# Two of the eight modulation groups of a diffusion trunk's first stage: off TensorE, onto VectorE and onto ScalarE with GpSimd

## The chip, the cores and the metric

The kernel runs on one core of a Trainium2 chip. The metric is the device time of one execution in microseconds, as the median over runs. Engines are named as in the profile: PE is TensorE (matmul; PEld its weight loads), DVE is VectorE, ACT is ScalarE, POOL is GpSimd, SP is the engine that issues most DMAs.

## The reference

The reference is a trunk of two layers over 512 latent tokens and 256 context tokens, width 2048, all in float32. Each layer normalises its input, scales and shifts it by vectors that come from a condition, and projects it. The part that matters here is the modulation of the first layer:

```python
c_act = jax.nn.silu(c)
cc_act = jax.nn.silu(c_ctx)
...
shift, scale, gate = jnp.split(c_act @ w_mod + b_mod, 3, axis=-1)
shift_c, scale_c, gate_c = jnp.split(cc_act @ w_mod + b_mod, 3, axis=-1)
...
hc = rms_norm(xc, norm_g) * (1 + scale_c) + shift_c
h = rms_norm(x, norm_g) * (1 + scale[:, None, :]) + shift[:, None, :]
p = h @ w_in
```

So two vectors of 2048 (one for latent, one for context tokens) are multiplied by the first 4096 columns of `w_mod` (2048 x 6144), 33.5 MB that are read once. Everything after it (pooling, neighbourhood attention, convolution, output projection) is left as it is by the change.

## The kernel before

`start` (L531) is the first stage. It loads x and the context, transposes them, and makes the first four blocks of the projection `h @ w_in` with the class `Multi` (L1583), eight PSUM accumulators at a time. The 16 slices k of h (128 channels each) become available two at a time, since slice k needs its shift and scale.

*Modulation groups.* `mod_first` (L338) makes the shift and scale of one pair of slices, j and j + 1: group j, for j = 0, 2, ... 14. A group has 16 tiles of `w_mod` of 128 x 512 floats (256 KB, L347), issued by SP into a ring of `WB` = 27 buffers with the tag `wm`. PE multiplies four tiles at a time, each in its own 32 columns of the array (L353, one *step*); four steps make a group. The trace has two records per tile, so a step is a row of x8. Then `row` copies the PSUM row to SBUF with DVE and ACT (L358, L359), and `columns` lets PE sum the four parts and turn the row into columns (L364, the *fold*), whereupon DVE adds the bias (L407 to L409).

*The modulate chain.* Behind the fold, `modulate` (L626) makes the two latent and two context slices: DVE multiplies (L632), ACT adds the shift and rounds to the high part (L636, `hil` or `hic`), DVE makes the low part (L637). DVE and ACT alternate, four times per group.

*The order.* Every engine executes its instructions in the order in which the Python code records them. `mod_order` puts the steps, rows and folds of the eight groups into one list `work`. For each pair of slices, `Multi.unit` runs over four blocks and calls `between` twice per block, after the latent and after the context matmuls: 8 x 4 x 2 = 64 *places*. At each place `between` (L675) takes as many entries of `work` as a table (`xs`, `ys`) says, so that group j's fold stands 7 places ahead of the pair that needs it (group 10's at place 33, group 12's at 41, group 14's at 49). A step is recorded with the loads of later tiles behind it (`load`), into the buffers which it frees.

*Weights.* The weight tiles `raw` of `w_in` (256 KB, L254) are loaded by SP in the same queue, converted by ACT (L298), and their low part made by POOL (L300) in this stage. Three matmuls per slice use them (`mm3`, L734 to L736).

*The later modulation.* `mod_rest` makes the gate and the second layer's modulation off PE already: DVE multiplies and adds (`mac`, L369 to L377), and `mod_sum` (L380) sums over partitions with eight matmuls (L384), `mod_row` copies (L390), and `mod_columns` transposes (L396).

Of the kernel before, what the change touches and what calls it, by code (L numbers as in the profile page):

```python
# [10 lines left out]
F32 = mybir.dt.float32  # L11
F32R = mybir.dt.float32r
I32 = mybir.dt.int32
AF = mybir.ActivationFunctionType
ALU = mybir.AluOpType
# [4 lines left out]
D = 2048  # L20
KT = 16
# [11 lines left out]

CONV_K = 31
NMULTI = 4
RAW = 4

MORE = (1, 3)
# [54 lines left out]
class Kernel:  # L93
# [84 lines left out]
    def setup(self):  # L178
# [21 lines left out]
        for l in range(2):  # L200
            bl = self.blocks(l)
            for u in range(4):
                self.order += [("in", l, col, u) for _, col, _ in bl[:NMULTI]]
            for name, col, _ in bl[NMULTI:]:
                if name not in "qkvg":
# [70 lines left out]
    def w_conv(self):  # L276
# [11 lines left out]
        else:  # L288
# [8 lines left out]
            else:  # L297
                nc.scalar.activation(out=hi, in_=t, func=AF.Copy)  # L298
                eng = nc.gpsimd if n < 4 * NMULTI else nc.vector
                eng.tensor_tensor(out=lo, in0=t, in1=hi.bitcast(F32), op=ALU.subtract)  # L300
# [36 lines left out]
    def mod_first(self, p, j, bufs):  # L337
# [29 lines left out]

        return ([lambda k=k: load(k) for k in range(KT)], [lambda k=k: mm(k) for k in range(0, KT, 4)], [row, columns])

    def mac(self, acc, wm, k):  # L370

        for r, a in enumerate(acc):
            w = self.cond[:, r, k:k + 1]
            if k == 0:
                self.nc.vector.tensor_scalar(out=a, in0=wm, scalar1=w, scalar2=None, op0=ALU.mult)
            else:
                self.nc.vector.scalar_tensor_tensor(out=a, in0=wm, scalar=w, in1=a, op0=ALU.mult, op1=ALU.add)  # L377
# [7 lines left out]
                                      start=r == 0, stop=r == len(acc) - 1)  # L385
        return ps

    def mod_row(self, p, ps):
        ms = p.tile([128, 128], F32, tag="ms", name="ms")
        self.nc.vector.tensor_copy(out=ms, in_=ps[:, :128])  # L390
        return ms

# [138 lines left out]

    def start(self, p):
        nc = self.nc
        WB = 27

        work = self.mod_order(p, WB, lambda k, cx: modulate(k, cx))
        loads = deque(f for w in work for f in w[0])

        def load(n=1):
            for _ in range(min(n, len(loads))):  # L540
                loads.popleft()()
# [4 lines left out]
        for c in range(4):  # L546
            for cx, c1 in ((False, c), (True, 2 * c), (True, 2 * c + 1)):
                for tb in (4, 5) if cx else range(4):
                    w = 256 if cx else 512
                    key = ("c" if cx else "l") + str(2 * c1 + tb - 4 if cx else 4 * c1 + tb)  # L550
                    t = self.ph.tile([128, w], F32, tag="hi" + key, name="x" + key)
                    src = self.ctx_in[0, (tb - 4) * 128:(tb - 3) * 128] if cx else self.x[0, tb * 128:(tb + 1) * 128]
# [2 lines left out]
        load(8)  # L555
        while self.n_load < RAW:
            self.w_load()
        load(12)
        self.cs = p.tile([128, KT, 32], F32, name="cs")
        self.zero = p.tile([128, 128], F32R, name="zero")  # L560
        nc.gpsimd.memset(self.cs, 0.0)
# [1 line left out]
        for r in range(2):  # L563
# [4 lines left out]
                                op=ALU.add)  # L568
# [79 lines left out]
                    if j == "row":  # L648
                        break

        load(WB - 20)
        go(2)

        nc.vector.tensor_reduce(out=self.st[:, 0, 0:6], in_=ssq, axis=AX.X, op=ALU.add)
        r = self.rstd(self.st[:, 0, 0:6], 6, 1.0 / D, EPS)
        rb = p.tile([128, NT], F32, name="rb")
        for a, n in ((0, 4), (4, 2)):
            d = p.tile([128, 128 * n], F32, tag="junk0", name="diag")
# [11 lines left out]
        total, i = len(work), 0  # L670
# [5 lines left out]
        def between():  # L676
            nonlocal i
            i += 1
            go(int(np.interp(i, xs, ys)) - total + len(work))

        for j in range(0, KT, 2):
            while j not in done:
                go()
            for b in range(NMULTI):
                m.unit(j // 4, b, (j, j + 1), between)
        return m

    def mod_order(self, p, bufs, modulate):

        work = deque()  # L690
        for j in range(0, KT, 2):
            ld, mm, (row, columns) = self.mod_first(p, j, bufs)
            work.extend((ld[4 * n:4 * n + 4], f, None) for n, f in enumerate(mm))
            work.append(((), row, "row"))

            def finish(j=j, columns=columns):
                columns()
                for cx in (False, True):
                    for k in (j, j + 1):
                        modulate(k, cx)  # L700

            work.append(((), finish, j))
        return work
# [959 lines left out]
```

## Time and profile before

| | |
|---|---|
| median of 3 runs | 2376.94 us (2376.27 to 2379.21) |
| the profiled execution | 2379.58 us, its span 2377.8 us |
| PE busy | 2333.8 us, 98% of the span |
| DVE, ACT, POOL busy | 1577.4, 907.7, 525.4 us |
| DMA | 384.96 MB, mean 162 GB/s; 316 and 343 GB/s in the first two of 40 slices (59 us each) |

The span is cut into 40 slices on the page; the first stage, of which the change speaks, fills the first two and most of the third. Busy time of PE is modelled, so a full PE need not be PE at its peak. Where a wait is put down to an engine, that is the one that came last by the profile.

### The profile page before, as it was taken

The numbers are of one execution on the slowest core, as the hardware profiler recorded it, in microseconds if no ns is written. First come the engines' busy times: TensorE is split into PE (matmuls) and PEld (weight loads), VectorE is DVE, ScalarE is ACT, GpSimd is POOL, SyncE is SP. The second block draws the span as 40 slices with busy tenths as digits, with TensorE's granted clock in tenths as the row PEclk, the third lists the DMA queues.
The fourth block names the chain that finished last, engine by engine and source line by source line (L and its number), as shares of the span: only waits on it lengthen the run. The fifth ranks groups of instructions, "written<-read, shape, count | busy, mean of one in ns | idle before, by whom it ended". The sixth has DMA issues, their size and how long they took to land. (4 is left out here: it accounts for less than half of the span.)

```text
span 2377.8 us, 35567 instructions
## 1 busy us (share of the span) xinstructions
PE 2333.8 (98%) x13020; PEld 1976.9 (83%) x13020; DVE 1577.4 (66%) x2815; ACT 907.7 (38%) x1798; POOL 525.4 (22%) x654
## 2 busy tenths in 40 slices
PE   7999999999999999999999999999999999999998
PEld 4578888888888888888787887878888888888888
DVE  4359995468777877877666387863666667555435
ACT  4233335233333333344522265544333334344323
POOL 1124554122212212211101122452111111010001
PEclk9999999999999999999999999999999999999999
DMA  9967787556355435535765347986555554334633
GB/s 316 343 184 186 166 209 165 154 149 160 99 152 152 137 103 157 159 100 165 240 205 164 125 148 172 207 183 162 150 139 138 149 146 127 102 89 123 202 120 129
DMA packets 377072, 384.96 MB, mean 162 GB/s; under 512 B 24672, under 2 KB 294080, under 8 KB 376768
## 3 DMA queue, kind: packets, MB, share of 16 engines
q1 hardware_dynamic: 339232, 290.92, 41.8%
q0 software_dynamic: 37664, 91.76, 16.8%
q8 instruction: 102, 1.67, 0.3%
q14 instruction: 74, 0.61, 0.1%
HBM read 296.57 MB, written 24.08 MB: 135 GB/s over the span
## 5 line engine op out<-in xcount | busy, mean ns | idle before, releaser
L734 PE MATMUL g<-hil,whi 128*128 128x512 f32 x1600 | 634.5, 397 | 0.0
L736 PE MATMUL g<-hil,wlo 128*128 128x512 f32 x1600 | 626.2, 391 | 6.3 <-DMA wlo<-raw 4.0
L735 PE MATMUL g<-lol,whi 128*128 128x512 f32 x1600 | 627.1, 392 | 0.0
L300 DVE TENSOR_TENSOR wlo<-raw,whi 128x512 fp32r<-128x512 f32 x424 | 308.7, 732 | 181.3 <-ACT whi L298 178.3
L298 ACT ACTIVATE whi<-raw 128x512 fp32r<-128x512 f32 x440 | 272.9, 625 | 359.0 <-PE g L735 125.9
L736 PEld LDWEIGHTS g<-hil,wlo 128*128 128x128 f32 x1600 | 300.8, 188 | 75.5 <-DMA wlo<-raw 5.9
L377 DVE SCALAR_TENSOR_TENSOR mod<-wm,cond,mod 128x512 f32<-128x512 f32 x420 | 338.6, 847 | 26.2 <-DMA wm<-in_w_mod_dram 25.8
L734 PEld LDWEIGHTS g<-hil,whi 128*128 128x128 f32 x1600 | 301.7, 189 | 60.0 <-issue 6.8
L735 PEld LDWEIGHTS g<-lol,whi 128*128 128x128 f32 x1600 | 301.7, 189 | 53.1 <-issue 1.4
L736 PE MATMUL g<-hic,wlo 128*128 128x256 f32 x1024 | 290.0, 283 | 0.0
L735 PE MATMUL g<-loc,whi 128*128 128x256 f32 x1024 | 289.9, 283 | 0.0
L734 PE MATMUL g<-hic,whi 128*128 128x256 f32 x1024 | 288.6, 282 | 0.0
L839 DVE SCALAR_TENSOR_TENSOR acc<-ypad,cols,acc 128x783 f32<-128x783 f32 (+1 forms) x240 | 241.6, 1007 | 7.4
L734 PEld LDWEIGHTS g<-hic,whi 128*128 128x128 f32 x1024 | 195.4, 191 | 9.4
L735 PEld LDWEIGHTS g<-loc,whi 128*128 128x128 f32 x1024 | 195.5, 191 | 9.3
L736 PEld LDWEIGHTS g<-hic,wlo 128*128 128x128 f32 x1024 | 195.5, 191 | 0.0
L1239 ACT ACTIVATE e<-e,m 128x512 f32<-128x512 f32 x128 | 92.6, 724 | 249.0 <-DVE m L1237 249.0
L295 POOL DMA_DIRECT2D wlo<-raw x128 | 114.7, 896 | 253.0 <-ACT wlo L294 213.5
L432 POOL DMA_DIRECT2D wm<-in_w_mod_dram x98 | 71.2, 726 | 340.3 <-DVE mod L377 256.3
L294 ACT ACTIVATE wlo<-raw 128x512 fp32r<-128x512 f32 x128 | 80.4, 628 | 127.3 <-PE g L736 122.2
L1463 POOL TENSOR_TENSOR xn<-xn,res 128x512 f32<-128x512 f32 (+1 forms) x34 | 45.9, 1358 | 332.4 <-DVE xn L1459 270.6
L434 POOL DMA_DIRECT2D wm<-in_w_mod_dram x88 | 48.3, 549 | 249.8 <-DVE mod L377 218.4
(324 smaller groups left out, 3812.9 us busy)
## 6 DMA issues: line engine op xcount, KB each, us to landing
raw<-in_w_in_dram SPq DMA_DIRECT2D x416, 256.0 KB, 3.8
wm<-in_w_mod_dram SPq DMA_DIRECT2D x198, 256.0 KB, 5.9
wm<-in_w_mod_dram POOLq DMA_DIRECT2D x186, 256.0 KB, 4.1
raw<-in_w_out_dram SPq DMA_DIRECT2D x160, 256.0 KB, 3.2
wlo<-raw POOLq DMA_DIRECT2D x128, 256.0 KB, 4.5
q<-parts SPq DMA_DIRECT2D x32, 384.0 KB, 8.7
k<-parts SPq DMA_DIRECT2D x64, 192.0 KB, 3.9
raw<-mixd SPq DMA_DIRECT2D x32, 256.0 KB, 3.1
```

Source lines behind the costliest of these rows:

```text
L294: nc.scalar.activation(out=lo, in_=t, func=AF.Copy, scale=-1.0)
L295: nc.gpsimd.dma_start(out=lo, in_=t, accum_op=ALU.add)
L298: nc.scalar.activation(out=hi, in_=t, func=AF.Copy)
L300: eng.tensor_tensor(out=lo, in0=t, in1=hi.bitcast(F32), op=ALU.subtract)
L377: self.nc.vector.scalar_tensor_tensor(out=a, in0=wm, scalar=w, in1=a, op0=ALU.mult, op1=ALU.add)
L432: self.wm_queue.dma_start(out=t.rearrange("p (s n) -> p s n", s=2), in_=src)
L434: self.wm_queue.dma_start(out=t, in_=rows[:, 2 * D + 512 * j:2 * D + 512 * j + 512])
L734: mm(ps, whi, hhi, start=start, stop=False)
L735: mm(ps, whi, hlo, start=False, stop=False)
L736: mm(ps, wlo, hhi, start=False, stop=stop)
L839: nc.vector.scalar_tensor_tensor(out=acc[i][:, 0:na], in0=y[:, j:j + na], scalar=w, in1=acc[i][:, 0:na], op0=ALU.mult, op1=ALU.add)
L1239: nc.scalar.activation(out=e, in_=e, func=AF.Exp, scale=-1.0, bias=m[:, 0:1], accum_out=m[:, 1:2])
```

## The change

Group 12 is summed by DVE (`"d"` in the table `SIDE`), group 14 by ACT and POOL (`"p"`). The new `mod_side` loads their 32 tiles with the name `ws`, through rings of 4 and 3 buffers, on SP. DVE takes two instructions per tile (one per condition, with `mac`). For the other group ACT writes two products per tile and POOL adds each to its sum. Both end with `mod_sum`, `mod_row` and `mod_columns`, as in `mod_rest`. Step k of a side group stands at place `int(at[k]) + 1`, evenly from 1 to 34 for group 12 and from 1 to 42 for group 14. Its four steps and fold on PE are gone; row and columns of both groups stay in `work`, which puts the sum matmuls at places 37 and 45 and the transposes at 41 and 49. The ring `wm` shrinks from 27 to 14 buffers, and two prefetches (`load(12)`, `load(WB - 20)`) become one (`load(6)`).

```diff
--- before.py
+++ after.py
@@ -33,6 +33,8 @@
 
 CONV_K = 31
 NMULTI = 4
+
+SIDE = {12: "d", 14: "p"}
 RAW = 4
 
 MORE = (1, 3)
@@ -367,6 +369,41 @@
 
         return ([lambda k=k: load(k) for k in range(KT)], [lambda k=k: mm(k) for k in range(0, KT, 4)], [row, columns])
 
+    def mod_side(self, p, j, eng, name):
+
+
+        nc = self.nc
+        bufs = 4 if eng is nc.vector else 3
+        wm, s = {}, {}
+        acc = [p.tile([128, 512], F32, name=f"{name}{r}") for r in range(2)]
+
+        def load(k):
+            if k < KT:
+                t = wm[k] = p.tile([128, 512], F32, tag=name, name="ws", bufs=bufs)
+                src = self.w_mod[0, k * 128:(k + 1) * 128, 0:2 * D].rearrange("p (s n) -> p s n", s=2)
+                nc.sync.dma_start(out=t.rearrange("p (s n) -> p s n", s=2), in_=src[:, :, 128 * j:128 * (j + 2)])
+
+        def step(k):
+            if k == 0:
+                for i in range(bufs - 1):
+                    load(i)
+            load(k + bufs - 1)
+            if eng is nc.vector:
+                self.mac(acc, wm.pop(k), k)
+                return
+            t = wm.pop(k)
+            for r in range(2):
+
+                x = p.tile([128, 512], F32, tag="wq", name="wq", bufs=2) if k else acc[r]
+                nc.scalar.activation(out=x, in_=t, func=AF.Copy, scale=self.cond[:, r, k:k + 1])
+                if k:
+                    eng.tensor_tensor(out=acc[r], in0=acc[r], in1=x, op=ALU.add)
+
+        def row():
+            s["ms"] = self.mod_row(p, self.mod_sum(acc), "ms" + name)
+
+        return ([lambda k=k: step(k) for k in range(KT)], [row, lambda: self.mod_columns(0, j, s["ms"], "t")])
+
     def mac(self, acc, wm, k):
 
         for r, a in enumerate(acc):
@@ -385,8 +422,8 @@
                                       start=r == 0, stop=r == len(acc) - 1)
         return ps
 
-    def mod_row(self, p, ps):
-        ms = p.tile([128, 128], F32, tag="ms", name="ms")
+    def mod_row(self, p, ps, tag="ms"):
+        ms = p.tile([128, 128], F32, tag=tag, name="ms")
         self.nc.vector.tensor_copy(out=ms, in_=ps[:, :128])
         return ms
 
@@ -531,7 +568,7 @@
 
     def start(self, p):
         nc = self.nc
-        WB = 27
+        WB = 14
 
         work = self.mod_order(p, WB, lambda k, cx: modulate(k, cx))
         loads = deque(f for w in work for f in w[0])
@@ -555,7 +592,7 @@
         load(8)
         while self.n_load < RAW:
             self.w_load()
-        load(12)
+        load(6)
         self.cs = p.tile([128, KT, 32], F32, name="cs")
         self.zero = p.tile([128, 128], F32R, name="zero")
         nc.gpsimd.memset(self.cs, 0.0)
@@ -648,7 +685,6 @@
                     if j == "row":
                         break
 
-        load(WB - 20)
         go(2)
 
         nc.vector.tensor_reduce(out=self.st[:, 0, 0:6], in_=ssq, axis=AX.X, op=ALU.add)
@@ -678,6 +714,12 @@
             i += 1
             go(int(np.interp(i, xs, ys)) - total + len(work))
 
+            for n, steps in enumerate(self.side):
+                at = np.linspace(0, 33 + 8 * n, KT)
+                for k in range(KT):
+                    if i - 1 == int(at[k]):
+                        steps[k]()
+
         for j in range(0, KT, 2):
             while j not in done:
                 go()
@@ -688,9 +730,14 @@
     def mod_order(self, p, bufs, modulate):
 
         work = deque()
+        self.side = []
         for j in range(0, KT, 2):
-            ld, mm, (row, columns) = self.mod_first(p, j, bufs)
-            work.extend((ld[4 * n:4 * n + 4], f, None) for n, f in enumerate(mm))
+            if j in SIDE:
+                steps, (row, columns) = self.mod_side(p, j, {"d": self.nc.vector, "p": self.nc.gpsimd}[SIDE[j]], "w" + SIDE[j])
+                self.side.append(steps)
+            else:
+                ld, mm, (row, columns) = self.mod_first(p, j, bufs)
+                work.extend((ld[4 * n:4 * n + 4], f, None) for n, f in enumerate(mm))
             work.append(((), row, "row"))
 
             def finish(j=j, columns=columns):
```

Counted from the first modulation tile, the 96th and last tile of groups 0 to 10 was SP's load 108 (96 of them and 12 of weights); now it is load 136 (96, 27 side tiles and 13 of weights). The 128 tiles and 16 weight tiles of the stage end with load 144 before, and the last side tile is load 144 now.

The queue of SP, before, from the loads behind group 0's last two steps on (`raw` weights, `wm` modulation tiles):

```order
L347 DMA wm<-in_w_mod_dram 128x2x256 x8
L254 DMA raw<-in_w_in_dram 128x4x128
L347 DMA wm<-in_w_mod_dram 128x2x256 x32
L254 DMA raw<-in_w_in_dram 128x4x128
L347 DMA wm<-in_w_mod_dram 128x2x256 x8
L254 DMA raw<-in_w_in_dram 128x4x128
L347 DMA wm<-in_w_mod_dram 128x2x256 x4
```

And now, from the loads behind group 2's steps on (`ws` are side tiles):

```order
L349 DMA wm<-in_w_mod_dram 128x2x256 x16
L384 DMA ws<-in_w_mod_dram 128x2x256 x7
L349 DMA wm<-in_w_mod_dram 128x2x256 x4
L384 DMA ws<-in_w_mod_dram 128x2x256 x2
L349 DMA wm<-in_w_mod_dram 128x2x256 x8
L384 DMA ws<-in_w_mod_dram 128x2x256 x2
L349 DMA wm<-in_w_mod_dram 128x2x256 x4
L384 DMA ws<-in_w_mod_dram 128x2x256 x3
L256 DMA raw<-in_w_in_dram 128x4x128
```

Side tiles now stand among the tiles of groups 4 to 10; 27 of the 32 are ahead of the last of these.

DVE around group 10's chain, before: the end of the chain (`lol`, `loc` low parts), then the copy of group 12's row and its bias:

```order
L637 SCALAR_TENSOR_TENSOR lol_1280<-xm,sh_78,hil_1279 128x512
L632 SCALAR_TENSOR_TENSOR xm<-xTc_406,gs_76,rb 128x256
L637 SCALAR_TENSOR_TENSOR loc_1286<-xm,sh_78,hic_1285 128x256
L632 SCALAR_TENSOR_TENSOR xm<-xTc_408,gs_76,rb 128x256
L637 SCALAR_TENSOR_TENSOR loc_1292<-xm,sh_78,hic_1291 128x256
L358 COPY ms<-pv 128x256
L407 TENSOR_TENSOR sh_78<-t,cols 128x2x2
```

And now, up to the copy of group 12's summed row (L427, of what PE's sum matmuls wrote):

```order
L674 SCALAR_TENSOR_TENSOR lol_1388<-xm,sh_78,hil_1387 128x512
L669 SCALAR_TENSOR_TENSOR xm<-xTc_398,gs_76,rb 128x256
L674 SCALAR_TENSOR_TENSOR loc_1394<-xm,sh_78,hic_1393 128x256
L669 SCALAR_TENSOR_TENSOR xm<-xTc_400,gs_76,rb 128x256
L674 SCALAR_TENSOR_TENSOR loc_1400<-xm,sh_78,hic_1399 128x256
L414 SCALAR_TENSOR_TENSOR wd_93<-ws,cond,wd_93 128x512
L414 SCALAR_TENSOR_TENSOR wd_94<-ws,cond,wd_94 128x512
L427 COPY ms<-pv 128x128
```

The last two products of the side sum (`wd`, L414) stand behind the whole chain, and ahead of the row that PE sums from them.

ACT around group 12's chain, before (`hil` and `hic` high parts, `ms` a row, `whi` weights):

```order
L359 ACTIVATE ms<-pv 128x256
L636 ACTIVATE hil_1383<-xm,sh_78 128x512
L636 ACTIVATE hil_1389<-xm,sh_78 128x512
L636 ACTIVATE hic_1395<-xm,sh_78 128x256
L636 ACTIVATE hic_1401<-xm,sh_78 128x256
L298 ACTIVATE whi<-raw 128x512 x3
L359 ACTIVATE ms<-pv 128x256
L298 ACTIVATE whi<-raw 128x512
L636 ACTIVATE hil_1507<-xm,sh_78 128x512
```

And now (`wq` the products that POOL adds):

```order
L398 ACTIVATE wq<-ws,cond 128x512 x6
L673 ACTIVATE hil_1493<-xm,sh_78 128x512
L673 ACTIVATE hil_1499<-xm,sh_78 128x512
L673 ACTIVATE hic_1505<-xm,sh_78 128x256
L673 ACTIVATE hic_1511<-xm,sh_78 128x256
L398 ACTIVATE wq<-ws,cond 128x512 x2
L300 ACTIVATE whi<-raw 128x512 x4
L673 ACTIVATE hil_1611<-xm,sh_78 128x512
```

The products of the last tile stand behind the four high parts of group 12, and the row copies of groups 12 and 14 on ACT are gone.

## Rows read from the trace of the kernel before

**Rows 1.** The page, part 1: busy time and share of the span.

```profile
PE 2333.8 (98%) x13020; PEld 1976.9 (83%) x13020; DVE 1577.4 (66%) x2815; ACT 907.7 (38%) x1798; POOL 525.4 (22%) x654
```

**Rows 2.** By stretch: length, busy engines, granted PE clock, DMA share, GB/s.

```profile
46.00:50.00 4.00, 4.00 (x8) 2.20 (x8) 2.64 (x5) 1.23 (x2) 0.00 (x0) 0.50 1.11 349
50.00:54.00 4.00, 4.00 (x33) 1.11 (x32) 1.19 (x3) 1.03 (x2) 1.28 (x1) 0.81 1.11 344
62.00:67.00 5.00, 4.75 (x20) 1.53 (x17) 1.36 (x3) 0.55 (x2) 0.00 (x0) 1.00 1.10 336
67.00:81.00 14.00, 14.00 (x89) 8.67 (x88) 5.19 (x12) 3.05 (x6) 0.00 (x0) 1.00 1.10 348
137.00:151.00 14.00, 14.00 (x88) 11.32 (x85) 5.51 (x12) 4.98 (x10) 5.04 (x4) 1.00 0.26 76
```

**Rows 3.** Timeline of SP, first stage: start, length, loads in a row.

```profile
29.41 20.36 SPq L347 DMA_DIRECT2D wm<-in_w_mod_dram  x27
...
59.85 23.82 SPq L347 DMA_DIRECT2D wm<-in_w_mod_dram  x32
...
100.28 11.60 SPq L347 DMA_DIRECT2D wm<-in_w_mod_dram  x16
...
127.53 3.53 SPq L347 DMA_DIRECT2D wm<-in_w_mod_dram  x5
```

**Rows 4.** Waits of SP's queue, 0 to 150: total us, times, longest.

```profile
SPq L347 <- DMA wm<-in_w_mod_dram: 28.2, 86, 0.8
...
SPq L347 <- PE pv L353: 5.6, 13, 1.1
```

**Rows 5.** Timeline of PE: wm steps (L353), folds (L364), first matmuls of pairs.

```profile
50.06 4.32 PE L353 MATMUL pv<-wm,cs 128*32 128x512 f32 x32
...
100.57 0.95 PE L364 MATMUL t<-fold,ms 128*128 128x2 f32 x8
...
111.42 1.07 PE L353 MATMUL pv<-wm,cs 128*32 128x512 f32 x8
...
114.63 0.95 PE L364 MATMUL t<-fold,ms 128*128 128x2 f32 x8
...
152.04 0.28 PE L734 MATMUL s<-hic,whi 128*128 128x256 f32 x1
...
160.44 0.39 PE L734 MATMUL g<-hil,whi 128*128 128x512 f32 x1
```

**Rows 6.** Timelines of PE and PEld: two waits, length and releaser.

```profile
45.92 0.80 PE L1601 MATMUL s<-hil,zero 128*128 128x512 f32 x1 [2.16 <-ACT hil L636]
...
65.97 0.14 PEld L353 LDWEIGHTS pv<-wm,cs 128*32 128x32 f32 x2 [1.16 <-DMA wm<-in_w_mod_dram]
```

**Rows 7.** PE timeline later; lines by form, 0 to 150; two lines (min/median/max).

```profile
285.68 0.64 PE L384 MATMUL pv<-mod,sel 128*32 128x128 f32 x16
286.25 0.50 PE L734 MATMUL g<-hil,whi 128*128 128x512 f32 x1
...
686.40 0.27 PE L396 MATMUL pv<-kc,ms 128*128 128x128 f32 x1
...
L300 POOL TENSOR_TENSOR wlo<-raw,whi 128x512 fp32r<-128x512 f32 x16 | 20.1, 1275 | 121.7 <-ACT whi L298 93.5 <-DMA wm<-in_w_mod_dram 28.3
...
L298 ACT ACTIVATE whi<-raw 128x512 fp32r<-128x512 f32 x16 | 9.4, 621 | 0.3
...
L377 DVE SCALAR_TENSOR_TENSOR mod<-wm,cond,mod x420: 737/746/3495, 174.1 to 2020.3; 128x512 f32<-128x512 f32 x140
...
L788 POOL TENSOR_TENSOR pwl<-pw,pwh x8: 1401/1582/1636, 203.0 to 1518.4; 128x512 fp32r<-128x512 f32 x8
```

**Rows 8.** Timelines of DVE and ACT: ends of one modulate chain.

```profile
115.61 0.17 DVE L407 TENSOR_TENSOR sh<-t,cols 128x4 f32<-128x4 f32 x1 [2.55 <-PE t L364]
...
123.01 0.48 DVE L637 SCALAR_TENSOR_TENSOR loc<-xm,sh,hic 128x256 fp32r<-128x256 f32 x1 [0.58 <-ACT hic L636]
...
122.47 0.51 ACT L636 ACTIVATE hic<-xm,sh 128x256 fp32r<-128x256 f32 x1 [0.95 <-DVE xm L632]
```

## Prediction

> **What bounds the kernel now.** I read the page first: PE is busy for 98% of the span [rows 1], so once the first stage is over whatever shifts PE shifts the end, and only the first 160 us need a closer look. Next came the busy time by stretch [rows 2]. The DMA share is at 1.10 to 1.11 with 336 to 349 GB/s in the stretches from 46 to 81 us, and in 137:151, when the modulation tiles are in, it falls to 0.26. So two things are at their limit in the same stage: PE, full from 67 us on, and the transfers, full until about 135 us.
>
> The queue of SP, in order of time, shows the same from the side of the loads [rows 3]. Count loads from the first modulation tile. Load 52 goes out at 59.85, and the 32 loads of that row take 23.82 us, 0.744 us each. Load 144, the last modulation tile, starts 0.37 us before its row ends, at 130.69: 92 intervals in 70.84 us, 0.770 each. SP spends 28.2 us in 86 waits for earlier modulation transfers and 5.6 us in 13 waits for PE to free a buffer [rows 4]: the transfers set the pace.
>
> PE's rows [rows 5] show how close PE runs behind. One group takes 14.06 us (fold at 100.57 to fold at 114.63). A pair of k without modulation work takes 8.40 us (152.04 to 160.44). So a group's four steps and its fold cost PE 5.66 us. Tile 44 was load 52, issued at 59.85, and PE's wait for it ended at 65.97 [rows 6]: landing is 6.1 us behind the issue. Tile 96, the last of group 10, is load 108, the fifth of the row at 100.28, so issued near 103.3 and landed near 109.4. PE begins that step at 111.42. The slack is 2 us.
>
> **The change, part by part.**
> *Work off PE.* Groups 12 and 14 lose eight steps and two folds: 2 x 5.66 = 11.3 us less. Each gets 16 sum records, 0.57 us from their start to the next matmul, and one transpose of 0.27 us [rows 7]: 2 x 0.84 = 1.7 us more. All of it is in PE's queue, so all of it counts: -9.6 us.
>
> *Order of the loads.* The bytes stay the same; their order does not. Steps of the side groups stand at places 1 to 34 and 1 to 42 of the stage's 64, and the paces of groups 0 to 10 are kept. So 27 side tiles and one more weight tile now go out ahead of tile 96: it is load 136, not 108. The sums that need these side tiles stand later, at places 37 and 45. Three groups (tiles 48 to 95) now span 73 loads, 24.3 per group, 18.2 us at 0.75, where PE needs 14.06: PE waits about 4 us in each. Landing of tile 96 from load 52: 65.97 + 84 x 0.75 = 129.0. To this comes the smaller ring: group 2's four steps stand together, beginning at 50.06 and lasting 4.32 us [rows 5]. Load 39 would go out at 29.41 + 26 x 0.754 = 49.0 [rows 3], but with 14 buffers it waits for the first of these steps, near 51.1. I put 2.1 us, bounds 0 and 4. So tile 96 lands near 131.1 and its step ends some 1.1 us later, at 132.2, where it ended at 111.42 + 1.07 = 112.5 before: **+19.7 us**. Bounds: 65.97 + 84 x 0.744 without the ring gives +17; 109.4 + 28 x 0.770 with it gives +21.6.
>
> Row against rule: the rows move one 256 KB load in 0.744 to 0.770 us, 340 to 352 GB/s. The Trainium skill (DMA: Bandwidth & Descriptors, Specifications) gives two ceilings, 358 GB/s for HBM per core and 435 GB/s for the fabric. By the first the 28 loads would cost 20.5 us, by the second 16.9, in place of 21.0; the rows sit just under the first.
>
> *First new wait: the VectorE sum.* Its last products (k = 15) stand behind the whole modulate chain of group 10 in DVE's order, and the sum matmuls stand four places after that group's fold. The chain runs from 0.98 us after the start of a fold (114.63 to 115.61) until 123.49 [rows 5, 8], 8.86 us after it. Two products at 0.746 us [rows 7] end at 10.4. PE needs 0.95 us for the fold and half of 8.40 for four places, so it arrives at 5.1. It waits **5.3 us**. Queued behind it is all of PE's order.
>
> *Second new wait: the ACT and GpSimd sum.* Its last products stand behind the chain of group 12 in ACT's order. The last hic of a chain ends at 122.98 [rows 8], 8.35 us after the fold began; a transpose is 0.68 us shorter than a fold, so 7.7 us after it. Two ACT products at 0.62 us and two adds at 1.27 us, the second add behind the first: 7.7 + 0.62 + 2.54 = 10.9. PE arrives 0.27 + 4.20 = 4.5 us after the transpose began. It waits **6.4 us**. The other 14 sum steps lie beside waiting time: 2 x 0.746 on DVE and 2 x 1.27 on POOL per tile, against over 5 us between steps.
>
> Row against rule: a POOL add of this size takes 1275 ns where DVE stands idle beside it, 1582 in the next stage where DVE is full [rows 7]. The Trainium skill (GPSIMD Engine Reference, 8. Key points) says that GpSimd shares its SBUF interfaces with VectorE and contends with instructions of two SBUF inputs, which the products are. With 1582 ns the second wait is 7.0 us; I keep 1275, since DVE has finished the chain when the last adds run.
>
> *The clock.* Behind a wait of 2.16 us that ended at 45.92 [rows 6] PE was granted 0.50, the lower of its levels (1.2 GHz), in 46:50 and 0.81 on average in 50:54 [rows 2]: 4 x 0.50 + 4 x 0.19 = 2.8 us lost. The new waits are longer. I count 2.4 after the first (of that loss, since the work up to the transpose is only some 4.8 us) and 2.8 after the second: **+5.2**, bounds 0 and 7. In the stretch that waits for transfers I count nothing: in 62:67 PE waited 1.16 us at once [rows 6] and kept 1.00 [rows 2].
>
> *Nothing else.* GpSimd's 30 adds and ACT's 32 products are covered by the engines' idle time; if that cover went, the second wait would grow, not a new one come. SP's waits for side buffers fall where the ring is already behind the transfers.
>
> Sum: 19.7 - 9.6 + 5.3 + 6.4 + 5.2 = **+27.0 us**. The profiled execution took 2379.58 us (span 2377.8); it would take 2406.6. It lies 2.6 us above the median of the three runs shown, so I forecast 2376.94 + 27.0 = **2404 us**.
>
> **Rivals.**
> 1. *Only the transfers' order costs.* If DVE's and ACT's last products were through before PE arrives, the two waits and their clock go: 19.7 - 9.6 = +10.1, 2387. Against it: the order puts them behind chains of 8.9 and 8.35 us [rows 8], for it only that a PE slowed by the clock arrives later. Chance 0.12.
> 2. *The transfers have room (not slower).* If the early side tiles hid, PE would keep its 14.06 us per group and the 19.7 would go. Then -9.6 + 5.3 + 6.4 = +2.1 without a clock loss, 2379: no change. The point that decides is whether 24.3 loads land in 14.06 us, 0.579 us each or 453 GB/s; no stretch shows over 349 [rows 2]. SP's waits for transfers [rows 4] speak against it too; for it, only that PE's step waits all but end after 66 us. Chance 0.10, 0.04 of it faster than the bound, since the two waits may be partly hidden then.
> 3. *The queue stalls as well.* SP issues in order: a side load waits for the product three or four tiles back, and behind it stand the tiles of groups 4 to 10. If each of the three modulate chains in that stretch holds SP long enough to empty the ring, some 4 us each, and PE falls to half clock there, the sum rises by 12 and more: 2416 to 2422. For it: ACT comes out of a chain 9.7 us after the fold, about when SP gets to the load behind it. Against it: some 15 loads are allowed and not landed at that moment. Chance 0.10.
>
> **How the numbers follow.** The forecast case has 0.68 and, from its bounds (17 to 21.6, waits 11 to 13, clock 0 to 7), lies between 2393 and 2411. The range takes in rival 1: **2385 to 2412**; rival 2 and most of rival 3 are left out. About 0.2%, 5 us, is what a measurement of this kernel tells from no change. Faster 0.04, same 0.06, slower 0.90.
>
> **What would show it.** In the changed profile: steps of groups 4 to 10 waiting for modulation tiles, about 4 us a group, and the fold of group 10 near 134 us in place of 114.63; a PE wait for DVE of about 5 us at the first sum and for POOL of 6 us at the second; a granted clock under 1 behind each; the DMA share near 1.1 until about 130 us; the conv stage beginning near 187 us rather than 160.44. It is wrong if the fold of group 10 comes before 125 us, or if no PE wait stands at the sums.

## The result, and the profile after

The changed kernel takes 2434.03 us (median of four runs, 2430.29 to 2435.26), the kernel before 2378.07 in the same job: ratio 1.0228, 95% interval 1.0216 to 1.0241. It is **56 us slower**; the forecast was 27 us slower and a range up to 2412. The profiled execution took 2435.26 us, its span 2433.4. Line numbers of the changed kernel are 2 higher than before up to the fold (L366), 37 higher behind it; in the experiments they shift by another line or two.

The page, part 1, of the kernel after, beside [rows 1]:

```profile
PE 2351.8 (97%) x12974; PEld 1987.1 (82%) x12974; DVE 1620.6 (67%) x2847; ACT 928.6 (38%) x1828; POOL 573.5 (24%) x684
```

PE is still busy nearly throughout, but its idle time (span less busy) has grown from 44.0 to 81.6 us, and its modelled busy time by 18.0 us although it has less to do. Its timeline shows that the loss is in the first stage (start, length, tile, count, and in brackets the wait with its releaser), folds and sums:

```profile
92.24 1.87 PE L366 MATMUL t<-fold,ms 128*128 128x2 f32 x8 [9.94 <-DVE ms L360]
111.77 3.26 PE L355 MATMUL pv<-wm,cs 128*32 128x512 f32 x4 [5.29 <-DMA wm<-in_w_mod_dram]
118.33 0.95 PE L366 MATMUL t<-fold,ms 128*128 128x2 f32 x8
136.68 1.05 PE L366 MATMUL t<-fold,ms 128*128 128x2 f32 x8
160.48 0.95 PE L366 MATMUL t<-fold,ms 128*128 128x2 f32 x8
170.16 0.66 PE L421 MATMUL pv<-wd,sel 128*32 128x128 f32 x8 [4.42 <-DVE wd L414]
171.74 0.65 PE L421 MATMUL pv<-wd,sel 128*32 128x128 f32 x8 [0.93 <-DVE wd L414]
187.77 0.65 PE L421 MATMUL pv<-wp,sel 128*32 128x128 f32 x8 [5.21 <-POOL wp L400]
188.99 0.65 PE L421 MATMUL pv<-wp,sel 128*32 128x128 f32 x8 [0.57 <-POOL wp L400]
```

The folds are of groups 4, 6, 8 and 10. The last, at 160.48, answers to 114.63 in [rows 5]: 46 us later, where I expected 134. The two waits at the sums are there, about as long as I had them (4.42 + 0.93 and 5.21 + 0.57 us). Nothing announced the 9.94 us in the first row.

By stretch (length, busy engines, granted PE clock, DMA share, GB/s), beside [rows 2]:

```profile
80.00:100.00 20.00, 10.06 (x51) 7.47 (x54) 14.57 (x20) 6.11 (x11) 6.62 (x4) 0.74 0.68 216
98.00:106.00 8.00, 8.00 (x52) 4.05 (x44) 6.48 (x8) 4.24 (x8) 3.79 (x3) 1.00 0.01 2
100.00:120.00 20.00, 14.71 (x69) 8.14 (x62) 13.11 (x16) 7.25 (x13) 14.99 (x10) 0.83 0.56 175
120.00:140.00 20.00, 18.88 (x99) 10.14 (x102) 15.26 (x20) 7.68 (x12) 10.07 (x6) 1.00 1.11 343
140.00:160.00 20.00, 14.02 (x66) 6.27 (x63) 16.55 (x16) 8.44 (x14) 14.17 (x9) 0.83 0.69 218
```

I had taken the transfers for the pace setter, at a share of 1.1 until 130 us. They run dry instead: 2 GB/s for 8 us from 98 on. SP's waits (0 to 260 us: total, times, longest) and its timeline say why:

```profile
SPq L256 <- POOL wlo L302: 56.8, 10, 19.7
...
89.55 3.21 SPq L384 DMA_DIRECT2D ws<-in_w_mod_dram  x3
107.25 0.37 SPq L256 DMA_DIRECT2D raw<-in_w_in_dram  x1
```

For 14.5 us, from 92.76 to 107.25, SP stands at one weight load (L256), whose buffer GpSimd's low part (L302) must free; every modulation tile is queued behind it. GpSimd's timeline shows where that low part stood: behind sums (L400), which waited for ACT's products.

```profile
102.21 3.34 POOL L400 TENSOR_TENSOR wp<-wp,wq 128x512 f32<-128x512 f32 x2 [11.57 <-ACT wq L398]
105.51 1.71 POOL L302 TENSOR_TENSOR wlo<-raw,whi 128x512 fp32r<-128x512 f32 x1
```

VectorE's timeline explains the wait of 9.94 us:

```profile
62.51 0.42 DVE L360 COPY ms<-pv 128x256 f32<-128x256 f32 x1 [9.99 <-PE pv L355]
72.96 0.88 DVE L412 TENSOR_SCALAR wd<-ws,cond 128x512 f32<-128x512 f32 x2 [10.03 <-DMA ws<-in_w_mod_dram]
73.76 0.16 DVE L444 TENSOR_TENSOR sh<-t,cols 128x4 f32<-128x4 f32 x1
...
83.77 8.09 DVE L414 SCALAR_TENSOR_TENSOR wd<-ws,cond,wd 128x512 f32<-128x512 f32 x6
91.78 0.41 DVE L360 COPY ms<-pv 128x256 f32<-128x256 f32 x1
```

Group 2's row copy is done at 62.93, but the columns' sums (L444) stand behind the first product, and that waits 10 us for its tile. Then the chain, then six products that take 8.09 us together, and only then group 4's row copy, for which PE waits. A product here is longer than the 0.746 us of [rows 7]. Lengths in the stage, min/median/max in ns:

```profile
L414 DVE SCALAR_TENSOR_TENSOR wd<-ws,cond,wd x30: 740/1749/1784, 83.8 to 169.9; 128x512 f32<-128x512 f32 x30
L400 POOL TENSOR_TENSOR wp<-wp,wq x30: 1257/1704/1742, 84.0 to 187.7; 128x512 f32<-128x512 f32 x30
```

So there are three suspects beside the terms of the forecast: **SP held** at weight loads, the **first side tile**, and the **length of the work** in VectorE's and GpSimd's queues.

### The profile page after: what moved, and what is told of

It is laid out like the page before. It is cut to its first block, busy times and chain, and to the rows that moved or that the text cites. A ratio compares the mean times of both kernels' runs of the same rounds, so it can differ in the third digit from the quotient of the medians.

```text
span 2433.4 us, 35578 instructions
## 1 busy us (share of the span) xinstructions
PE 2351.8 (97%) x12974; PEld 1987.1 (82%) x12974; DVE 1620.6 (67%) x2847; ACT 928.6 (38%) x1828; POOL 573.5 (24%) x684
## 5 line engine op out<-in xcount | busy, mean ns | idle before, releaser
L302 DVE TENSOR_TENSOR wlo<-raw,whi 128x512 fp32r<-128x512 f32 x424 | 310.6, 736 | 185.2 <-ACT whi L300 182.3
L414 DVE SCALAR_TENSOR_TENSOR mod<-wm,cond,mod 128x512 f32<-128x512 f32 x420 | 335.9, 841 | 25.1 <-DMA wm<-in_w_mod_dram 24.4
```

## The experiments

Times are medians; the kernel before was timed with each job (2378 to 2380), and "+" is the excess over it.

**Parts of the change alone.** First the ring of 14, with its shorter prefetch, without side groups:

```diff
-SIDE = {12: "d", 14: "p"}
+SIDE = {}
```

> No side group at all: all eight groups on PE as before, but the ring of 14 buffers and its prefetch. The prediction's 2 us (bounds 0 and 4) for the ring: 2376 to 2382. If the smaller ring lets the transfers run dry in every group, 5 us and more per group, it is above 2400 and the main cause by itself.

2403.47, **+23.4**, ratio 1.0096 (1.008 to 1.0113). My 2.1 us was ten times too small. SP's waits and timeline in this run:

```profile
SPq L256 <- POOL wlo L302: 35.9, 6, 9.7
...
69.70 8.65 SPq L349 DMA_DIRECT2D wm<-in_w_mod_dram  x12
87.19 0.37 SPq L256 DMA_DIRECT2D raw<-in_w_in_dram  x1
```

It is the weight load again, 8.8 us. In the kernel before, the same load went out at 84.06 us, right behind the 32 tiles that end at 83.67 [rows 3]. SP's only waits there for low parts, 10.8 us in 4 times (0 to 150 us), all fall between 131 and 150 us, behind the last modulation tile, where they hold up no tile of the eight groups:

```profile
SPq L254 <- POOL wlo L300: 10.8, 4, 7.5
...
138.95 4.97 SPq L254 DMA_DIRECT2D raw<-in_w_in_dram  x4
```

With 14 buffers the load has 62 modulation tiles ahead of it in the queue, not 75. SP comes to it at 78.35, stands until 87.19, and the prefetched tiles run out behind it.

Then one group alone (`SIDE = {12: "d"}`, `SIDE = {14: "p"}` on its own 42 places), and the change with its transfers but products and sums cut to one column from the second tile on:

> Group 12 on DVE alone, group 14 on PE as before, ring of 14. Theory C: without POOL's sums the products take 0.75 us again, and the fold of group 10 comes some 30 us earlier than in the changed kernel. Theory A: DVE still waits about 10 us for the first side tile ahead of a modulate chain, but SP's 14 us gap for a raw weight is gone, since POOL has nothing else to do; near 2395. Theory B: 14 side tiles ahead of tile 96 in place of 27, so about half of 19.7 us at the fold of group 10, less 4.8 us of PE work, plus the first new wait of 5 us: near 2386.

> Group 14 on ACT and POOL alone, at its places of the changed kernel, group 12 on PE as before, ring of 14. Theory C: POOL's adds take 1.3 us where DVE is idle and slow down only beside the modulate chains; little beyond theory B. Theory A: the gap of SP for a raw weight stays in part, since POOL's low parts still stand behind its adds and these behind ACT's chain, 5 to 10 us per four weight tiles: near 2400. Theory B: 13 side tiles ahead of tile 96, near 2387 with the second new wait of 6 us.

> The changed kernel with the same loads in the same order, but from the second tile of each side group on DVE, ACT and POOL work on one column of 512 only (so the modulation of groups 12 and 14 is not the reference's). Theory B (the order of the transfers alone, the prediction's first term): the fold of group 10 near 134 us, the kernel some 10 us slower than before, near 2388. Theory A (queues that block each other: side products ahead of the modulate chain and of the row copy on DVE and ACT, raw loads behind POOL's low parts): the waits for the first side tile stay, 10 us on DVE, and the fold of group 10 comes near 140, the kernel near 2395. Theory C (DVE and POOL slow each other: 1.75 us per product in place of 0.75): nearly all beyond theory B goes with the work, so as theory B. If none of these, and it stays above 2420, the loads themselves block SP.

2416.42 (+36.3), 2414.92 (+34.8) and 2409.18 (+29.1). All three lie 14 to 21 us above the slowest of their theories, none of which had the ring's price. Each group costs 11 to 13 us beyond the ring, both together 33; without most of their work the change keeps 29 of its 56. The lengths of the work when one engine does it alone, VectorE's in the first run and GpSimd's in the second:

```profile
L414 DVE SCALAR_TENSOR_TENSOR wd<-ws,cond,wd x30: 737/746/1782, 80.0 to 153.8; 128x512 f32<-128x512 f32 x30
```

```profile
L400 POOL TENSOR_TENSOR wp<-wp,wq x30: 1262/1272/1299, 80.5 to 173.4; 128x512 f32<-128x512 f32 x30
```

Medians of 746 and 1272 alone, 1749 and 1704 together: **the two engines slow each other**. The Trainium skill (SBUF — State Buffer, Who interferes with whom) says that a VectorE instruction with two SBUF inputs contends with a GpSimd one that reads SBUF. The rows agree. The summary table of the same page of the Trainium skill (Summary: rules for kernel authors) has the second fully blocked until the first ends; by that a product and a sum would take 0.746 + 1.272 = 2.02 us in turns, but both come every 1.7 us, so here they overlap in part.

**SP freed.** The first stage's weight loads from the fifth on go out from GpSimd's queue, right behind the low part that frees their buffer:

```diff
-            self.nc.sync.dma_start(out=t.rearrange("p (k n) -> p k n", k=4), in_=self.w_src(a, b, l))
+            q = self.nc.gpsimd if RAW <= self.n_load < RAW + 4 * NMULTI else self.nc.sync
+            q.dma_start(out=t.rearrange("p (k n) -> p k n", k=4), in_=self.w_src(a, b, l))
```

> No side groups, ring of 14; the first stage's weight loads from the fifth on (16 of them) are issued from GpSimd's queue, behind the low part that frees their buffer, in place of SP's. The ring of 14 alone measured 2403.5, some 23 us above the kernel before. Theory 'SP is held': these 23 us are SyncE standing at a weight load until GpSimd's low part frees the raw buffer, while the modulation loads queued behind it could run. Then 2380 to 2387, no stretch of 8 us without a load issued on SP, and the fold of group 6 back near 87 us from 98. Theory 'too shallow': 14 tiles can't bridge the modulation's bursts whoever issues the weights; then 2398 to 2405 with the folds where the ring of 14 alone has them.

2381.95, **+2.5** (ratio 1.0012, 1.0003 to 1.0022). SP's row from 70 us on is not broken by a weight load any more; its longest wait in it is 4.0 us, for PE to free a buffer:

```profile
70.22 64.31 SPq L350 DMA_DIRECT2D wm<-in_w_mod_dram  x72
```

So 14 tiles are nearly deep enough: 21 of the ring's 23 us are SP standing at a load that waits for another engine. That is shown: the fold of group 6 also comes back, from 98.45 to 86.99 us, 86.51 before. The same on the full change:

> The change in full, with the first stage's weight loads from the fifth on issued from GpSimd's queue behind the low parts. 'SP is held': SP no longer stands at weight loads (56.8 us of such waits in the change), the modulation loads keep moving, and most of the 23 us comes back: 2408 to 2418; it still waits for the side tiles' buffers. 'Too shallow': 2428 to 2436. 'GpSimd is the bound' (the low parts stand behind the sums whoever issues the loads, so the weights are as late as before and PE waits for them): 2425 to 2436, with SP's waits gone all the same.

2433.73, no gain at all (+54.3). That is inside the ranges of two theories, but PE waits neither for a tile as long as before nor for weights. PE's waits (30 to 230 us) of the change, and then of this run:

```profile
PE pv L355 <- DMA wm<-in_w_mod_dram: 17.6, 9, 6.0
PE t L366 <- DVE ms L360: 10.5, 2, 9.9
```

```profile
PE t L367 <- DVE ms L361: 27.2, 5, 8.3
...
PE pv L356 <- DMA wm<-in_w_mod_dram: 4.7, 3, 3.3
```

The wait for tiles shrank by 12.9 us and the wait for VectorE's row copy grew by 16.7: two limits lie side by side, and taking one away shows the other. But the edit also has a price of its own on VectorE. The same six products in the change, then in this run, and GpSimd's timeline in this run:

```profile
101.95 9.16 DVE L414 SCALAR_TENSOR_TENSOR wd<-ws,cond,wd 128x512 f32<-128x512 f32 x6
```

```profile
99.29 15.45 DVE L415 SCALAR_TENSOR_TENSOR wd<-ws,cond,wd 128x512 f32<-128x512 f32 x6
...
104.88 0.76 POOL L257 DMA_DIRECT2D raw<-in_w_in_dram  x1 [0.29 <-POOL wlo L303]
105.66 2.52 POOL L401 TENSOR_TENSOR wp<-wp,wq 128x512 f32<-128x512 f32 x2
108.13 1.27 POOL L303 TENSOR_TENSOR wlo<-raw,whi 128x512 fp32r<-128x512 f32 x1
109.70 0.76 POOL L257 DMA_DIRECT2D raw<-in_w_in_dram  x1 [0.29 <-POOL wlo L303]
```

One product starts at 105.05, while GpSimd issues a weight load, and takes 4.91 us: until GpSimd issues the next. In the change no product takes over 1.79 us. This stretch is 6.3 us longer than in the change and the one ahead of group 10's fold 2.9 us (15.36 for 12.50), and behind these two PE's waits for the row copy are new (7.85 and 8.03 us). So up to 9.2 of the 16.7 us come with the edit, and what freeing SP alone would be worth in the full change is not shown. With a ring of 24, for which one group less leaves room, and weight loads on SP or on GpSimd:

> One side group (14, ACT's products and GpSimd's sums), group 12 back on PE, and the ring at 24, which the released buffers leave room for; with a ring of 14 the same measured 2414.9. 'The ring costs 23': a ring of 24 hides the wait at the weight loads again, so 2388 to 2400: the side group's own cost of some 11 us stays and PE's 4.8 us is won. 'SP is held by whatever waits': the side tiles' buffers and the later low parts hold SP long enough to use up 24 tiles too; then 2405 to 2415.

> Group 14 alone off PE, ring of 24, the first stage's weight loads from the fifth on issued by GpSimd. The same with these loads on SP measured 2408.2, with SP held 42 us at them. 'SP is held': with one side engine VectorE has no products, so nothing else takes over, and the time falls to 2380 to 2392. 'GpSimd's queue is the next bound' (the low parts, and the weight loads behind them, stand behind 30 sums of 1.28 us, and the sums behind ACT's products): 2398 to 2408.

> Group 12 alone off PE (VectorE), ring of 24, weight loads by GpSimd. With a ring of 14 and these loads on SP the same measured 2416.4. 'SP is held': 2380 to 2392 if VectorE's products (948 ns each in that run, two a tile) lie beside other work. 'VectorE's queue' (row copies and chains behind the products): PE's waits for VectorE's row copy stay and the time is 2395 to 2408.

2408.18 (+28.7), 2414.33 (+34.4) and 2408.75 (+28.8): with group 14 the deeper ring is worth 6 us, as the second theory had it. Loads behind the sums in GpSimd's queue are 6 us worse than on SP, outside both expectations; PE waits there 12.2 us, and 10.3 with the loads on SP, for ACT's half of the row copy. With group 12 alone the two steps together bring 7.5, about the upper end of 'VectorE's queue'. In the last run VectorE waits 18.6 us for its first tile, since that is queued behind a longer prefetch:

```profile
76.03 0.88 DVE L413 TENSOR_SCALAR wd<-ws,cond 128x512 f32<-128x512 f32 x2 [18.55 <-DMA ws<-in_w_mod_dram]
```

**GpSimd's sums short.** The second operand and the result of each sum cut to one column, then with the weight loads by GpSimd as well:

```diff
-                    eng.tensor_tensor(out=acc[r], in0=acc[r], in1=x, op=ALU.add)
+                    eng.tensor_tensor(out=acc[r][:, 0:1], in0=acc[r][:, 0:1], in1=x[:, 0:1], op=ALU.add)
```

> The change with GpSimd's sums on one column of the 512 (group 14's modulation then holds its first product alone in the other columns); VectorE's sums, ACT's products, the loads and the order stay. 'The two engines slow each other': VectorE's products fall from 1497 ns to at most the 948 ns that they have with group 12 alone, and the low parts come early; 2412 to 2420. 'Order of the queues': the time hangs on what VectorE's products stand ahead of and on the first side tile's wait, not on their length; 2426 to 2434 even with short sums.

> The change in full, weight loads by GpSimd, and GpSimd's sums on one column (group 14 holds its first product alone in the other columns). Short sums alone gave 2422.5, the loads by GpSimd alone nothing (2433.7). 'Two bounds side by side' (SP held, and VectorE slowed by GpSimd's sums): both gone gives more than the sum, 2392 to 2406. 'One cause': the loads add nothing to short sums either, 2418 to 2426.

2422.54 (+43.1) and 2410.85 (+30.9), each between its two expectations. VectorE's products are back at a median of 746 ns in both. Freeing SP is now worth 12 us, where it was worth 2, within the noise, before; one product over 2 us is left, of four. And the row copy taken off VectorE (ACT copies both halves), in the full change with SP free:

> The change in full, weight loads by GpSimd, and the row copy of the PE groups on ACT in one piece, where VectorE did its first half. With the loads by GpSimd alone the time stayed at 2433.7 and PE's wait for VectorE's row copy rose from 10.5 to 27.2 us. 'VectorE's queue is the second bound': the row copy no longer stands behind products and chains, so 2408 to 2420. 'It is only the place where the lateness shows' (the columns' sums behind the fold are VectorE's too, and the chains behind them): 2426 to 2436.

2429.77 (+49.8), 4 us less than without and in the range of 'only the place': PE's wait moves on to ACT's copy (20.1 us) and to VectorE's sum (8.5). The place of the copy is at most a small part of the cause.

**The first side tiles early.** Their loads stand ahead of the ring's prefetch, right behind the first four weight tiles:

```diff
-            if k == 0:
-                for i in range(bufs - 1):
-                    load(i)
+        self.early += [lambda i=i: load(i) for i in range(bufs - 1)]
...
+        for f in self.early:
+            f()
         load(6)
```

> The change in full, with the first side tiles (3 and 2) loaded ahead of the ring's prefetch and not at the first place between blocks. 'The first side tile': VectorE's and ACT's waits for it (10.0 and 12.6 us) go, group 2's modulation starts 10 us sooner, but SP is still held at the weight loads behind GpSimd: 2422 to 2428. 'Products ahead of every chain', or SP, hides it: 2430 to 2436.

2423.99 (+44.5). The columns of group 2 follow its row copy again, and 11.5 us of the excess are gone. With SP free as well, and then with group 12 alone:

> The same and the first stage's weight loads issued by GpSimd. Each of the two waits can hide behind the other, so both must go. 'First tile and SP together': 2408 to 2418, and the rest (some 30 us over the kernel before) is the long products and sums in the queues. 'Products ahead of every chain' alone: 2426 to 2434.

> Group 12 alone on VectorE, ring of 24, weight loads by GpSimd (2408.75), and its first three tiles loaded ahead of the ring's prefetch. VectorE stood 18.6 us for the first of them. 'The first side tile': 2388 to 2396. 'Products ahead of every chain': 2403 to 2410, since six products of 0.7 us or more still stand ahead of each row copy.

> The same as the run before it, and the row copy of the PE groups on ACT in one piece, so that it stands behind no product. If the products ahead of the row copy still cost, 2376 to 2386, beside the kernel before or better; if that wait only moves to the chain on VectorE, the same time as the run before it, within 3 us.

2422.66 (+43.1), 2402.23 (+22.7) and 2398.41 (+18.9), each between its expectations, so none of the theories is borne out as it stands. In the first, freeing SP again brings 1 us, within the noise, and again PE only changes what it waits for, tiles without it (first fence), VectorE with it, where products of up to 4.93 us stand again:

```profile
PE pv L355 <- DMA wm<-in_w_mod_dram: 20.0, 7, 5.9
```

```profile
PE t L367 <- DVE ms L361: 18.7, 4, 8.2
```

None of these beats the kernel before. In the last one PE waits 11.9 us at once for VectorE's products at the sum. Group 12 alone had the ring of 24 only with the weight loads on GpSimd, and products of about 2.45 us go with these loads there too; the same with the loads on SP was not run.

**What the work itself costs.** Early tiles and SP free, with GpSimd's sums short, and then with the products short too:

> The same, but only GpSimd's sums on one column (group 14 holds its first product alone in the other columns); VectorE's and ACT's products are whole. Without the early tiles this measured 2410.9. 'First tile' and 'GpSimd's sums slow VectorE' add up: 2397 to 2403, so GpSimd's sums cost some 22 us and VectorE's and ACT's products the rest. If the early tiles are hidden here: 2407 to 2412.

> The change in full with early side tiles and weight loads by GpSimd (2422.7), and from the second tile on its products and sums on one column of 512 (groups 12 and 14 then hold their first product alone in the other columns); all transfers and places stay. 'The length of the work': 2378 to 2388, so order, ring and first tile are accounted for. 'The side tiles' buffers hold SP whatever the work' (3 or 4 buffers tie the transfers to VectorE's and ACT's place): 2395 to 2410.

2407.92 (+27.9) and 2403.28 (**+23.2**). The first falls to its rival: the early tiles are worth some 3 us here, not 10. The second has the time of the rival that I wrote against it, though not its mechanism, as the next rows show: 23 us remain with hardly any work. Its PE timeline, the fold of group 10 and the sums:

```profile
133.29 0.95 PE L367 MATMUL t<-fold,ms 128*128 128x2 f32 x8
142.82 1.08 PE L421 MATMUL pv<-wd,sel 128*32 128x128 f32 x16 [4.28 <-DVE wd L414]
...
157.37 1.08 PE L421 MATMUL pv<-wp,sel 128*32 128x128 f32 x16 [3.83 <-POOL wp L399]
```

and its stretches, transfers full until 120 us (share 1.07 to 1.10 from 40 us on):

```profile
100.00:120.00 20.00, 18.43 (x83) 9.03 (x85) 5.31 (x17) 4.07 (x11) 1.19 (x6) 1.00 1.10 343
...
140.00:160.00 20.00, 13.36 (x88) 11.11 (x89) 7.31 (x19) 6.36 (x17) 3.61 (x10) 0.82 0.05 14
160.00:180.00 20.00, 20.00 (x108) 17.32 (x107) 7.09 (x16) 8.90 (x17) 9.25 (x20) 0.92 0.31 77
```

The fold of group 10 at 133.29 is where the forecast put it (near 134). Ahead of tile 96 the side tiles' buffers hold SP for less than 1 us (60 to 125 us); with the transfers full, the pace is set by the 27 side tiles that go ahead of tile 96. The forecast's sum with this run's sizes: (133.29 - 114.63) - 9.6 + 4.28 + 3.83, and a clock of 0.82 and 0.92 in two stretches of 20 us (20 x 0.18 + 20 x 0.08 = 5.2, an upper estimate, since PE is idle for a third of the first), gives 22.4; measured 23.2 by the medians, 21.3 by the two profiled executions.

The excess falls step by step, each step on top of those ahead of it:

| kernel | excess, us | step |
|---|---|---|
| the change | 56.0 | |
| first side tiles early | 44.5 | -11.5 |
| and weight loads by GpSimd | 43.1 | -1.4 |
| and GpSimd's sums short | 27.9 | -15.2 |
| and products short | 23.2 | -4.7 |

The steps depend on their order: moving the weight loads to GpSimd is worth 21 where no side group stands, 12 with short sums, and 1 to 2, within the noise, where VectorE has full products beside full sums, which the loads make longer. Short sums are worth 12.9 on the change itself, 15.2 in this table, and 23.4 with the weight loads by GpSimd but late tiles; what these loads cost VectorE is part of the last two.

## Why the prediction was wrong

The direction was right, the size half of what came. The forecast's own terms are borne out where nothing else disturbs them: they leave 23.2 of the 56 us. Three steps failed: the ring at 2.1 us, the 14 sum steps "beside waiting time", and the first side tile's wait, which the sum does not have. Taken out one after the other, the first tile brought 11.5 us, the weight loads off SP 1.4, the shortened sums and products 19.9. Point by point:

- **Work off PE, order of the loads, the two new waits: right**, as far as runs show them. +19.7 for the loads (2.1 of it for the ring) measured 18.7 where nothing else disturbs them; 5.3 and 6.4 us at the sums measured 5.3 and 5.8 in the change. The first of these agrees by luck in part: the two products took 2.41 us beside GpSimd's sums, not 1.49, and half of PE's sum records ran beside the second. The -9.6 was not measured by itself.
- **The clock: too narrow.** I counted nothing in the stretch that waits for transfers, by one wait of 1.16 us [rows 6]. The change's longest waits there are 5 to 10 us long, and the granted clock is 0.74 and 0.83 in 80:100 and 100:120, where it was 1.00 before. From 40 to 200 us it is 0.74 to 0.83 in seven of the eight stretches of 20 us, before only in the first; 20 x (1 - clock) sums to 27.2 us there, 3.4 before. The difference of 24 is an upper estimate, since PE is idle in part of these stretches; what the clock cost by itself stays open.
- **The ring, "2.1, bounds 0 and 4": failed.** Alone it costs 23. I asked only when PE frees a buffer of the ring. What a deep ring did here was to keep SP so late that the weight loads in the same queue found their buffers free. The view of [rows 4] has SP's wait for GpSimd's low part, 10.8 us in 4 times, but behind the last tile: what had to be read was the place of the weight loads in the queue, 13 tiles earlier with the smaller ring. In the full change moving these loads brought nothing clear of the noise; how much of that is VectorE's queue and how much the price of the loads on GpSimd stays open.
- **"The other 14 sum steps lie beside waiting time": failed.** At 0.746 us the products nearly do (PE's wait for VectorE's row copy is 2.6 us with short sums, early tiles and SP free); at 1.7 and 1.7 six products fill 8 to 9 us, and eight 12.5, between a chain and the next group's row copy. I weighed the contention rule on the last sums alone, 0.6 us, and kept 1275 ns. The row was of a GpSimd instruction beside an idle VectorE, and the added work ends that idleness. Short sums are worth 12.9 us on the change. With early tiles and SP free they are worth 15.2, and there PE's wait for VectorE's row copy falls from 18.7 to 2.6 us with the products' median from 1763 to 747 ns, while PE's waits for tiles rise from 5.2 to 8.4: that gain goes through VectorE's queue. How it splits between the sums and the weight loads among them stays open, and so does the share of GpSimd's own queue in the 12.9.
- **Not seen at all: the first side tile.** In SP's order it lies behind the whole prefetched ring, in VectorE's and ACT's order ahead of group 2's columns and chain. It could be read from the order of the two queues: a load behind so many others, at 0.75 us each, can't have landed. Price 11.5 us in the change, 6 with group 12 alone, some 3 where the sums are short.
- **"Nothing else ... SP's waits for side buffers fall where the ring is already behind the transfers": half right.** These waits are small (7.3, 4.1 and 2.2 us for ACT, VectorE's products and its copy); SP's wait at the weight loads is 56.8. With the weight loads off SP, its waits for side buffers grow to 38 us (22.8, 9.7 and 5.4), while PE's wait for tiles is down to 4.7. GpSimd's sums stand ahead of the low parts, so the cover of ACT's and GpSimd's idle time was not free.
- Rival 3, "the queue stalls as well", was the nearest (2416 to 2422). It had SP held, but by side loads behind chains; "some 15 loads are allowed and not landed", my argument against it, counts loads that can't be issued while the queue's head waits.
- The signs that would have shown it wrong named only a fold that comes too early. A fold at 160 was as clear a sign, and the text had no word for it.
- The bounds given for the forecast case add up to 2395 and 2409, not to 2393 and 2411; against 2434 that changes nothing.

## What to carry to other kernels

Before a ring is made smaller, list everything in the same queue that waits for another engine's buffer: the ring's depth also pays for those waits, and here, without side groups, moving 16 weight loads to the engine that frees their buffers made 13 of 27 tiles (26 KB a partition) dispensable at +2.5 us. With VectorE busy the same move lengthened its products. Work moved to an in-order engine must be followed by name through that engine's queue: what its first instruction waits for, and what stands behind it. Price it with both engines running. When an experiment removes one wait without a gain, look for the wait that took its place, and for what the experiment itself added, before calling the first harmless.

## What the runs showed of the hardware

Neither of the two slowed engines is the winner: VectorE's products go from 746 to 1749 ns and GpSimd's sums from 1272 to 1704, so work spread over both gains little, 1.7 us a pair where turns would take 2.02.

A weight load issued from GpSimd's queue changes this. In the run with group 12 alone and the ring of 24, six products take 4.06 us with GpSimd idle and 8.54 us beside three low parts and the weight loads behind them:

```profile
84.63 4.06 DVE L415 SCALAR_TENSOR_TENSOR wd<-ws,cond,wd 128x512 f32<-128x512 f32 x6
...
98.78 8.54 DVE L415 SCALAR_TENSOR_TENSOR wd<-ws,cond,wd 128x512 f32<-128x512 f32 x6
```

GpSimd's timeline in that stretch:

```profile
98.95 1.71 POOL L303 TENSOR_TENSOR wlo<-raw,whi 128x512 fp32r<-128x512 f32 x1 [44.56 <-ACT whi L301]
100.96 0.76 POOL L257 DMA_DIRECT2D raw<-in_w_in_dram  x1 [0.29 <-PE pv L356]
101.74 1.31 POOL L303 TENSOR_TENSOR wlo<-raw,whi 128x512 fp32r<-128x512 f32 x1
103.35 0.76 POOL L257 DMA_DIRECT2D raw<-in_w_in_dram  x1 [0.29 <-PE s L785]
```

The first low part, without a load ahead of it, takes 1.71 us and the product beside it 1.77. The second follows a load and takes 1.31, about its length alone; the product that starts during the load (at 101.13) takes 2.48, until the next load. Behind a load in the full change the pattern is longer: two sums and a low part pass at about their length alone, and the product takes 4.91. In all the runs every product of the side sum of over 2 us starts while GpSimd issues a weight load and ends as it issues the next; where these loads are on SP, none takes over 1.8. Why a load has this effect is not shown. Such a load takes 776 ns of GpSimd, 12.4 us for the 16; without side groups the 16 cost at most the 2.5 us that the run lies above the kernel before.
